# First feed-forward projection as seven block products, second projection in groups of 8, 7 and 7 tiles

## The chip, the cores and the metric

The kernel runs on one core of a Trainium2 chip. The metric is device time in microseconds, the median of several runs. TensorE is PE here (its weight loads PEld), VectorE is DVE, ScalarE is ACT, GpSimd is POOL, and SyncE is SP, which issues most loads.

## The reference, cut to what matters

One layer of a transformer trunk for 512 latent and 128 context tokens, 640 in all, with D_MODEL = 1024 and D_FF = 2816. The change concerns its last part, after attention and the output projection:

```python
h = modulate(x, norm2_w, shift2, scale2)          # (640, 1024)
a, up = jnp.split(h @ w_ffn_in, 2, axis=-1)       # 2 x (640, 2816)
a = dwconv3(a, ffn_conv_w, ffn_conv_b)            # three neighbouring tokens
x = x + gate2[:, None, :] * ((jax.nn.silu(a) * up) @ w_ffn_out)
```

gate2 is a sixth of `silu(c) @ w_ada + b_ada`; a last RMSNorm with final_norm_w follows.

## The kernel before, in words

Everything is float32. A product is made of three TensorE products: each operand is split into a high part (rounded to the type fp32r) and the low rest, and hi x hi, hi x lo and lo x hi are added up in PSUM (`mm3`, `proj`; all matmuls are issued in `mm`, line 142). A weight tile is loaded by SP into one of three buffers `raw` (128 x 1024 columns, 512 KB), cast on ACT into `whi` (line 125) and subtracted on DVE into `wlo` (line 126); there are four buffers of each. The function `wload` does this.

Channels lie on partitions, tokens on columns. The feed-forward part takes 22 tiles of 128 channels. For a tile `ffn_proj` makes two projections, a (`pfa`) and up (`pfu`): eight blocks of 128 rows of h, three hi/lo terms, two token halves of 320 columns, 48 matmuls each. Then `ffn_tile` copies a out of PSUM (line 1088), applies the convolution (one ACT pass, line 1089; four DVE steps, lines 1091 and 1093, for latent and context tokens apart), SiLU (1095), the product with up (1096), and splits the result into gh and gl (1097, 1098). After 11 tiles the second projection adds them up into five token tiles (`acc`), in two passes of 512 output columns, and DVE multiplies by the gate and adds to x (lines 1171, 1172). So there are two groups of 11 tiles. The last pass of the second group calls `finish`, which also makes the last norm and stores.

The gate for this (`gate2`, in the profile `acc_g`) is made beside the first group: 8 loads of 512 KB of w_ada through the same `raw` buffers, 32 DVE accumulations of 512 columns (line 221), two splits and eight matmuls; `ffn` calls one step of it after each tile.

Ahead of it stands the output projection (`out_steps`, `pso`), 48 matmuls of 512 columns for each of five token tiles. A token tile's rows are then gated, added, normalised (lines 1026 to 1031), transposed on PE and modulated (`modulate`: evictions on DVE and ACT at lines 1046 and 1044, cast and subtraction into `h2` at 1050 and 1051). PE's order there is written out by hand and kept (`pinned`): the last modulation, of tile 4, comes after the first two half projections of the feed-forward part, which need only the first 320 tokens. From then on (`pinned[0] = False`) the framework's scheduler orders PE too; the other engines' order it always chooses itself, at compile time, from its own estimates, and every engine runs its instructions in order.

Of the kernel before, what the change touches and what calls it, by code (L numbers as in the profile page):

```python
# [67 lines left out]
def trunk_kernel(ctx: ExitStack, tc: tile.TileContext, a: dict, o: list):  # L68
# [41 lines left out]
    def f(ap):  # L110
        return ap.bitcast(F32)
# [29 lines left out]
    def mm(out, s, m, start, stop):  # L141
        pin(nc.tensor.matmul(out, s, m, start=start, stop=stop))  # L142
# [65 lines left out]
    def ada_acc(pool, col, hf, name):  # L208
# [3 lines left out]
        acc = pool.tile([P, 2, 512], F32, tag="acc", name=f"acc_{name}{hf}", bufs=2)  # L212
# [26 lines left out]
    def rows_cols(pool, ps):  # L239

        rows = pool.tile([8, 512], F32, tag="n2rows", name="n2rows", bufs=1)
# [731 lines left out]
    h2 = mg  # L973
    tail = ctx.enter_context(tc.tile_pool(name="tail", bufs=1, reuse_waits="tile"))
    x2 = [tail.tile([P, D], F32, tag=f"x2_{t}", name=f"x2_{t}") for t in range(NT)]
    g2 = [tail.tile([P, D], F32, tag=f"g2_{c}", name=f"g2_{c}") for c in range(2)]

    def ffn_half(i, u):

        w = wcols(w_fi, u * FF + i * P, P, 0, KD, f"f{'au'[u]}{i}")  # L980
        ps = bank2(f"pf{'au'[u]}{i}")
        proj(ps, w, h2, KD, halves=(0,))
        return ps, w

    def ffn_proj(i, u):
        if (i, u) in early or i < 2:
            ps, w = early.get((i, u)) or ffn_half(i, u)
            proj(ps, w, h2, KD, halves=(1,))
            return ps
        w = wcols(w_fi, u * FF + i * P, P, 0, KD, f"f{'au'[u]}{i}")  # L990
        ps = bank2(f"pf{'au'[u]}{i}")
        proj(ps, w, h2, KD)
        return ps

    early = {}
    with tc.tile_pool(name="wo", bufs=1, reuse_waits="tile") as wo:
# [3 lines left out]
        woB = [wo.tile([P, 3, D], F32R, tag=f"woB{i}", name=f"woB{i}") for i in range(2)]  # L1000

        def wo_of(i, k):
            return woA[i][:, k, :] if k < 5 else woB[i][:, k - 5, :]

        for k in range(KD):
            raw = wpool.tile([P, 1024], F32, tag="raw", name=f"raw_wo{k}", bufs=3)
            nc.sync.dma_start(raw, w_out[k * P:(k + 1) * P, :])
            nc.scalar.copy(wo_of(0, k), raw)
            nc.vector.tensor_tensor(wo_of(1, k), raw, f(wo_of(0, k)), ALU.subtract)
# [22 lines left out]

        def modulate(t):
            c, ts, y = t // 4, slice(t * P, (t + 1) * P), Y2[t]
            h32 = wo.tile([P, KD, P], F32, tag="h32", name=f"h32_{t}", bufs=1)
# [11 lines left out]
            n = KD if t < NT - 1 else KD // 2  # L1047
            for k in range(0, KD, n):
                ks = slice(k, k + n)
                nc.scalar.copy(h2[0][:, ks, ts], h32[:, ks, :])  # L1050
                nc.vector.tensor_tensor(h2[1][:, ks, ts], h32[:, ks, :], f(h2[0][:, ks, ts]), ALU.subtract)
# [20 lines left out]
    fw = ffn.tile([P, D], F32, tag="fw", name="fw", bufs=1)  # L1072
    nc.gpsimd.dma_start(fw, a["final_norm_w"].unsqueeze(0).broadcast_to([P, D]))
    GRP = 11

    def gate2():
        for hf in range(2):
            for acc in ada_acc(ffn, 5 * D, hf, "g2"):
# [4 lines left out]
    def ffn_tile(i, gh, gl):  # L1083
        pa, pu = (ffn_proj(i, u) for u in range(2))
        av = ffn.tile([P, TOK], F32, tag="av", name=f"av{i}", bufs=1)
        cv = ffn.tile([P, TOK], F32, tag="cv", name=f"cv{i}")
        w = [vcol[:, V_CW + j * NF + i:V_CW + j * NF + i + 1] for j in range(3)]
        nc.scalar.copy(two(av), pa[:, :, :HALF])
        nc.scalar.activation(two(cv), pa[:, :, :HALF], AF.Identity, bias=vcol[:, V_CB + i:V_CB + i + 1], scale=w[1])
        for s0, s1 in ((0, LAT), (LAT, TOK)):  # L1090
# [111 lines left out]
```

## Time and profile before

| | |
|---|---|
| median of 3 runs | 1108.32 us (1105.19 to 1108.43) |
| the profiled execution | 1108.31 us, span 1106.5 us |
| granted PE clock, mean | 0.991 |
| output projection, with its modulations | 578 to 638 us |
| feed-forward part, to the last matmuls of the second projection | 638 to 1100 us |

The profile is of one execution. Busy times are of instructions of an engine; a matmul's end is modelled, and matmuls overlap, so the time of one is read from the distance of their starts. A stretch's table tells which engine is full there, the chain of waits which work ended last. DVE's and POOL's instructions that wait for each other inside show that as a longer duration, not as idle time.

### The profile page before, as it was taken

To read this page: it belongs to the slowest core of one execution; us is meant where nothing else is said; L and a number is where in the kernel's file an instruction comes from. 1 tells how busy PE (TensorE), PEld (TensorE's weight loads), DVE (VectorE), ACT (ScalarE), POOL (GpSimd) and SP (SyncE) were. 2 spreads that over 40 slices of the span, in tenths; PEclk is the share of its full clock that TensorE was granted. 3 is DMA by queue.
4 is the path that set the end of the run, shared out by engine and by line. 5 is a ranking of instruction groups with operands and counts; after the bars stand their busy time and mean duration, and the time that the engine had idled before them with its cause. 6 is when DMAs were issued, how large, how long until landed. Compare 5 with 4: busy or idle time off the path is not lost.

```text
span 1106.5 us, 16752 instructions
## 1 busy us (share of the span) xinstructions
PE 1071.1 (97%) x6811; PEld 1006.3 (91%) x6811; DVE 701.2 (63%) x1041; ACT 486.5 (44%) x783; POOL 163.0 (15%) x160
## 2 busy tenths in 40 slices
PE   6988999999999999999999999999999999999997
PEld 4787899999999999999998899999988999999886
DVE  5968988988877577787756567564414444444164
ACT  8636667667665552222334444333311233333133
POOL 4444324323222630000000000000000000000020
PEclk9898999999999999999999999999999999999999
DMA  9830212112111124555565024241222222222212
GB/s 311 228 97 27 84 32 65 48 37 66 41 42 58 55 81 152 171 156 150 153 220 161 1 80 141 86 133 58 86 76 76 87 77 76 77 77 68 67 39 95
DMA packets 128478, 106.10 MB, mean 96 GB/s; under 512 B 4173, under 2 KB 110205, under 8 KB 128402
## 3 DMA queue, kind: packets, MB, share of 16 engines
q1 hardware_dynamic: 126450, 101.93, 29.9%
q0 software_dynamic: 1232, 1.80, 0.8%
q8 instruction: 53, 0.87, 0.3%
q10 hardware_dynamic: 720, 1.31, 0.3%
q14 instruction: 23, 0.19, 0.1%
HBM read 101.36 MB, written 3.67 MB: 95 GB/s over the span
## 4 chain that ended last, share of the span: by engine, by line
PE 80%; DVE 11%; ACT 4%; issue 2%; SPq 1%; DMA 1%; ACTq 0%; DVEq 0%
PE pfa L142 14%; PE pfu L142 14%; PE acc L142 13%; PE ps_g L142 10%; PE psyb L142 5%; PE pso L142 5%; PE psk L142 3%; PE psu L142 3%; PE psya L142 3%; PE s L142 2%; PE po L142 2%; PE psq L142 2%; DVE nm L667 2%; PE psv L142 2%; PE pat L145 1%
## 5 line engine op out<-in xcount | busy, mean ns | idle before, releaser
L142 PE MATMUL pfu<-mg,whi_fu 128*128 128x320 f32 x704 | 134.1, 308 | 0.0
L142 PE MATMUL pfa<-mg,whi_fa 128*128 128x320 f32 x704 | 134.1, 308 | 0.0
L142 PEld LDWEIGHTS pfa<-mg,whi_fa 128*128 128x128 f32 x704 | 110.9, 188 | 0.4
L142 PEld LDWEIGHTS pfu<-mg,whi_fu 128*128 128x128 f32 x704 | 110.7, 188 | 0.0
L142 PE MATMUL acc<-whi_fo,gA 128*128 128x512 f32 (+1 forms) x336 | 100.9, 379 | 0.0
L142 PE MATMUL ps_g<-hT,whi_g 128*128 128x320 f32 x512 | 96.7, 311 | 0.0
L142 PE MATMUL pfu<-mg,wlo_fu 128*128 128x320 f32 x352 | 82.2, 307 | 0.0
L142 PE MATMUL pfa<-mg,wlo_fa 128*128 128x320 f32 x352 | 82.2, 307 | 0.0
L142 PEld LDWEIGHTS ps_g<-hT,whi_g 128*128 128x128 f32 x512 | 80.2, 188 | 2.0 <-issue 1.5
L126 DVE TENSOR_TENSOR wlo_fo<-raw_fo,whi_fo 128x1024 fp32r<-128x1024 f32 (+1 forms) x24 | 27.3, 1145 | 80.8 <-ACT whi_fo L125 80.8
L669 ACT ACTIVATE p<-s,nm 128x640 f32<-128x640 f32 (+1 forms) x80 | 56.6, 709 | 40.0 <-DVE nm L667 39.4
L142 PEld LDWEIGHTS acc<-whi_fo,gA 128*128 128x128 f32 x336 | 62.1, 188 | 12.1
L126 DVE TENSOR_TENSOR wlo_fa<-raw_fa,whi_fa 128x1024 fp32r<-128x1024 f32 x22 | 26.9, 1224 | 66.3 <-ACT whi_fa L125 66.3
L1176 POOL TENSOR_TENSOR x<-x,fw 128x512 f32<-128x512 f32 x5 | 6.9, 1372 | 419.0 <-ACT sq L1175 419.0
L142 PE MATMUL psv<-whi_v,hT 128*128 128x256 f32 x320 | 66.4, 288 | 0.0
L125 ACT CAST whi_fo<-raw_fo 128x1024 fp32r<-128x1024 f32 (+1 forms) x24 | 23.3, 978 | 96.3 <-PE acc L142 71.3
L667 DVE TENSOR_REDUCE nm<-s 128x1 f32<-128x640 f32 (+1 forms) x80 | 56.5, 709 | 12.4 <-PE s L142 11.0
L142 PE MATMUL acc<-wlo_fo,gA 128*128 128x512 f32 (+1 forms) x168 | 63.7, 379 | 0.0
L125 ACT CAST whi_fa<-raw_fa 128x1024 fp32r<-128x1024 f32 x22 | 23.1, 1050 | 84.8 <-PE pfa L142 61.7
L221 DVE SCALAR_TENSOR_TENSOR acc_g<-raw_g,silu,acc_g 128x512 f32<-128x512 f32 x64 | 44.5, 746 | 24.8 <-DMA raw_g<-in_w_ada_dram 24.7
L142 PEld LDWEIGHTS pfu<-mg,wlo_fu 128*128 128x128 f32 x352 | 59.4, 188 | 0.0
L142 PEld LDWEIGHTS pfa<-mg,wlo_fa 128*128 128x128 f32 x352 | 59.4, 188 | 0.0
(337 smaller groups left out, 2576.3 us busy)
## 6 DMA issues: line engine op xcount, KB each, us to landing
raw_fa<-in_w_ffn_in_dram SPq DMA_DIRECT2D x22, 512.0 KB
raw_fu<-in_w_ffn_in_dram SPq DMA_DIRECT2D x22, 512.0 KB
raw_fo<-in_w_ffn_out_dram SPq DMA_DIRECT2D x20, 512.0 KB
raw_g<-in_w_in_dram SPq DMA_DIRECT2D x16, 512.0 KB
raw_g<-in_w_ada_dram SPq DMA_DIRECT2D x16, 512.0 KB
araw_sh<-in_w_ada_dram SPq DMA_DIRECT2D x8, 512.0 KB
araw_sc<-in_w_ada_dram SPq DMA_DIRECT2D x8, 512.0 KB
raw_v<-in_w_in_dram SPq DMA_DIRECT2D x8, 512.0 KB
```

Source lines behind the costliest of these rows:

```text
L125: nc.scalar.copy(hi[:, :n], rv)
L126: eng.tensor_tensor(lo[:, :n], rv, f(hi[:, :n]), ALU.subtract)
L142: pin(nc.tensor.matmul(out, s, m, start=start, stop=stop))
L145: pin(nc.tensor.transpose(out, x, ident))
L221: nc.vector.scalar_tensor_tensor(acc[:, c, :], raw[:, ki, :], sc[:, c, 2 * u + ki:2 * u + ki + 1], acc[:, c, :], ALU.mult, ALU.add)
L667: nc.vector.tensor_reduce(nm[:, i:i + 1], s, AX.XY, ALU.max, negate=True)
L669: nc.scalar.activation(p.rearrange("p (b n) -> p b n", b=s.shape[1]), s, AF.Exp, bias=nm[:, i:i + 1], accum_out=z[:, i:i + 1])
L1176: nc.gpsimd.tensor_tensor(x2[t][:, hs], x2[t][:, hs], fw[:, hs], ALU.mult)
```

## The change

The matrix [a; up] x [two halves of h's 1024 rows] x [two token halves] is taken as a 2 x 2 block product by Strassen's method in Winograd's form: seven products of (128 channels) x (512 rows) x (320 tokens) for a tile of a and up together, in place of eight. The sums of token blocks (`e1` to `e4`) are made once, in `modulate`; `e1` and the plain blocks go to `h2`, the others to the new `hx`. The sums of weight blocks are made for every tile on POOL (`weights2`) and then split on ACT and DVE like plain weights: `sa` for products 5 and 6, `sb` for 3 and 7. Products 1, 6, 7 and 4 add into one PSUM bank of a tile, 5 and 3 into its other, and 2 has its own; between them parts are copied out. `raw` buffers of a and up are now held until the sums have read them. The split of a's own weights is on POOL for tiles 0 to 7 and on DVE after. PE's order stays written out by hand to the end: `pinned` is not reset. In a tile's turn the products are (i,1), (i,2), (i-1,7), (i,5), (i,6), (i-1,4), (i,3). The groups are 8, 7 and 7 tiles, so that a group's results fit into the eight slots of two buffers; the second projection makes six passes in place of four, with the same matmuls in all, and its first two blocks come ahead of the group's last two products. The gate's steps all fall into the first group. The last three rows of w_out (`woB`) now lie in three of the four weight buffers.

The core of the diff:

```diff
-        for n, (i, u) in enumerate(((0, 0), (0, 1), (1, 0))):
-            if n == 2:
-                modulate(NT - 1)
-            early[i, u] = ffn_half(i, u)
-        pinned[0] = False
+        def weights2(i, p):
+            if p == 1:
+                raw2[i] = raw_of(i, 0)
+                hl = split(raw2[i], *w_pair(f"a{i}"), nc.gpsimd if i < GROUPS[1][0] else nc.vector)
+                W2[i, 1], W2[i, 2] = [x[:, :4, :] for x in hl], [x[:, 4:, :] for x in hl]
+            elif p == 5:
+                ra, ru = (raw2.pop(i) if i != 2 else raw_of(i, 0)), raw_of(i, 1)
+                sa, sb = (pools["ffn"].tile([P, KD, P], F32, tag="s", name=f"s{j}_{i}") for j in range(2))
+                nc.gpsimd.tensor_tensor(sa[:, :4, :], ru[:, :4, :], ru[:, 4:, :], ALU.add)
+                nc.gpsimd.tensor_tensor(sa[:, 4:, :], sa[:, :4, :], ra[:, :4, :], ALU.subtract)
+                hl = split(sa, *w_pair(f"s{i}"), nc.vector)
+                W2[i, 5], W2[i, 6] = [x[:, :4, :] for x in hl], [x[:, 4:, :] for x in hl]
+                nc.gpsimd.tensor_tensor(sb[:, :4, :], ra[:, 4:, :], sa[:, 4:, :], ALU.subtract)
+                nc.gpsimd.tensor_tensor(sb[:, 4:, :], ra[:, :4, :], ru[:, :4, :], ALU.subtract)
+                raw2[i] = ru
+                hl = split(sb, *w_pair(f"t{i}"), nc.vector)
+                W2[i, 3], W2[i, 7] = [x[:, :4, :] for x in hl], [x[:, 4:, :] for x in hl]
+            elif p == 7:
+                hl = [pools["ffn"].tile([P, 4, P], F32R, tag=t, name=f"{t}_{i}", bufs=1) for t in ("uh", "ul")]
+                W2[i, 4] = split(raw2.pop(i)[:, 4:, :], *hl, nc.gpsimd)
+        def product(i, p):
+            weights2(i, p)
+            if p == 1:
+                PS[i] = bank2(f"pf{i}")
+            pa, pc = PS[i][:, 0, :HALF], PS[i][:, 1, :HALF]
+            pb = bank1(f"pb{i}")[:, :HALF] if p == 2 else None
+            out = {1: pa, 6: pa, 7: pa, 4: pa, 5: pc, 3: pc, 2: pb}[p]
+            (wh, wl), (ah, al) = W2.pop((i, p)), h_block(p)
+            for k in range(4):
+                for n, (w, x) in enumerate(((wh, ah), (wh, al), (wl, ah))):
+                    mm(out, w[:, k, :], x[:, k, :], p in (1, 2, 5) and k + n == 0, k == 3 and n == 2, p in (6, 7, 4, 3))
...
+        for i, p in ((0, 1), (0, 2), (1, 1)):
+            product(i, p)
+        modulate(NT - 1)
+        product(2, 1)
...
+            for i, p in ((1, 2), (0, 5), (0, 6), (1, 5), (0, 3), (1, 6), (0, 7), (1, 3), (0, 4), (2, 2), (1, 7), (2, 5),
+                         (2, 6), (1, 4), (2, 3)):
+                product(i, p)
+                if p == 3:
+                    next(later, None)
...
+        for i in range(start, first + size):
+            for j, p in ((i, 1), (i, 2), (i - 1, 7), (i, 5), (i, 6), (i - 1, 4), (i, 3)):
+                product(j, p)
+            if g == 0:
+                next(later, None)
+                next(later, None)
...
+        out2 = out2_steps(g, 0)
+        for p in (7, 4):
+            next(out2)
+            product(end, p)
```

And in `modulate`, for the columns past the first 320 (`h1` holds the first 320 in float32):

```diff
+            nc.vector.tensor_tensor(e1, b12, h1[:, :4, cs], ALU.subtract)
+            nc.gpsimd.tensor_tensor(e3, b22, b12, ALU.subtract)
+            split_to(h2[0][:, :4, c2], h2[1][:, :4, c2], e1)
+            nc.vector.tensor_tensor(e2, b22, e1, ALU.subtract)
+            nc.gpsimd.tensor_tensor(e4, h1[:, 4:, cs], e2, ALU.subtract)
+            split_to(h2[0][:, 4:, c2], h2[1][:, 4:, c2], b22)
+            split_to(hx[0][:, :, cs], hx[1][:, :, cs], e[:, 4:, :n])
```

`split` and `split_to` are a cast on ACT and a subtraction on the engine named (DVE for `split_to`). After product 2 the corner is copied on ACT and added to on DVE, after 5 and 6 a part is copied out on ACT, after 3 and 7 a part is added on DVE. The convolution follows product 3; the product with up and the split into gh and gl follow product 4.

## Rows read from the trace of the kernel before

**Rows 1.** The page: busy us, share of the span and instructions of each engine.

```profile
PE 1071.1 (97%) x6811; PEld 1006.3 (91%) x6811; DVE 701.2 (63%) x1041; ACT 486.5 (44%) x783; POOL 163.0 (15%) x160
```

**Rows 2.** Table by stretch: length, busy us of PE, PEld, DVE, ACT, POOL; clock.

```profile
578.00:638.00 60.00, 60.00 (x281) 49.44 (x280) 34.24 (x49) 26.44 (x42) 0.00 (x0) 1.00 0.29 94
652.00:795.00 143.00, 143.00 (x975) 142.63 (x974) 81.49 (x116) 56.23 (x70) 0.00 (x0) 1.00 0.34 104
795.00:870.50 75.50, 75.50 (x333) 62.00 (x332) 23.06 (x28) 13.11 (x15) 0.00 (x0) 1.00 0.24 77
```

**Rows 3.** Chain of waits from 638 us: start, length, engine, tile, line, matmuls.

```profile
795.00 75.50 PE acc L142 x330
870.50 6.99 PE pfa L142 x48
877.49 6.99 PE pfu L142 x48
```

**Rows 4.** Groups by line, 690 to 1107 us: count, busy us, mean ns, idle before.

```profile
L126 DVE TENSOR_TENSOR wlo_fa<-raw_fa,whi_fa 128x1024 fp32r<-128x1024 f32 x17 | 20.8, 1224 | 57.4 <-ACT whi_fa L125 57.4
L125 ACT CAST whi_fa<-raw_fa 128x1024 fp32r<-128x1024 f32 x17 | 17.9, 1051 | 72.6 <-PE pfa L142 53.9 <-PE acc L142 12.2 <-PE pfu L142 6.5
L1091 DVE SCALAR_TENSOR_TENSOR cv<-av,vcol,cv 128x511 f32<-128x511 f32 x19 | 14.3, 751 | 2.6 <-ACT cv L1089 2.3
L1088 ACT COPY av<-pfa 128x640 f32<-128x640 f32 x18 | 12.3, 686 | 0.0
L1098 DVE TENSOR_TENSOR gA<-cv,gA 128x640 fp32r<-128x640 f32 x13 | 10.6, 819 | 0.0
L1091 DVE SCALAR_TENSOR_TENSOR cv<-av,vcol,cv 128x127 f32<-128x127 f32 x19 | 6.6, 346 | 0.0
L125 ACT CAST whi_fo<-raw_fo 128x512 fp32r<-128x512 f32 x4 | 2.5, 624 | 22.7 <-PE acc L142 22.7
L1109 DVE TENSOR_TENSOR yr<-acc,g 128x512 f32<-128x512 f32 x4 | 2.8, 689 | 9.1 <-PE acc L142 9.0
```

**Rows 5.** Timeline of DVE and of POOL, 1063 to 1069 us: start, length.

```profile
1064.22 1.78 DVE L1172 TENSOR_TENSOR x<-x,yr 128x512 f32<-128x512 f32 x1
...
1066.92 1.81 DVE L1172 TENSOR_TENSOR x<-x,yr 128x512 f32<-128x512 f32 x1
...
1063.75 1.70 POOL L1176 TENSOR_TENSOR x<-x,fw 128x512 f32<-128x512 f32 x1 [413.19 <-ACT sq L1175]
1066.90 1.29 POOL L1176 TENSOR_TENSOR x<-x,fw 128x512 f32<-128x512 f32 x1 [1.44 <-ACT sq L1175]
```

**Rows 6.** Timeline of POOL and of DVE in the attention part, 167 to 172 us.

```profile
167.94 2.41 POOL L126 TENSOR_TENSOR wlo_k<-raw_k,whi_k 128x1024 fp32r<-128x1024 f32 x1 [13.40 <-ACT whi_k L125]
170.30 1.80 POOL L541 TENSOR_TENSOR ry_k<-ry_k,cos 128x512 f32<-128x512 f32 x1
...
169.56 0.80 DVE L697 TENSOR_TENSOR tl<-pat,th 128x640 fp32r<-128x640 f32 x1
...
171.07 1.05 DVE L675 TENSOR_TENSOR z<-z,neglam 128x1 f32<-128x1 f32 x1
```

**Rows 7.** Timeline of DVE after the output projection: token tile 4's last row step.

```profile
643.35 0.75 DVE L1031 TENSOR_SCALAR y<-x,rstd_n 128x1024 f32<-128x1024 f32 x1
```

**Rows 8.** Timeline of SP and of ACT: a load of 512 KB and its cast.

```profile
592.35 0.37 SPq L122 DMA_DIRECT2D raw_fu<-in_w_ffn_in_dram  x1
...
596.06 1.05 ACT L125 CAST whi_fu<-raw_fu 128x1024 fp32r<-128x1024 f32 x1 [2.85 <-DMA raw_fu<-in_w_ffn_in_dram]
```

**Rows 9.** Table by stretch, columns as in rows 2: a hole of PE.

```profile
80.00:82.00 2.00, 0.00 (x0) 0.00 (x0) 1.97 (x2) 0.65 (x1) 1.91 (x2) 1.00 0.01 3
...
84.00:86.00 2.00, 0.00 (x0) 0.00 (x0) 1.97 (x2) 1.23 (x2) 1.63 (x1) 0.50 0.00 0
...
88.00:90.00 2.00, 2.00 (x10) 2.00 (x9) 1.76 (x3) 1.06 (x3) 0.00 (x0) 0.50 0.00 0
...
92.00:94.00 2.00, 2.00 (x16) 2.00 (x15) 1.94 (x3) 0.90 (x2) 1.94 (x2) 1.00 0.04 12
```

More of the change, by code (lines that the diff above doesn't have):

```diff
@@ L139, in pin, with mm @@
             tc.keep_in_program_order(ins)
-    def mm(out, s, m, start, stop):
-        pin(nc.tensor.matmul(out, s, m, start=start, stop=stop))
+    def mm(out, s, m, start, stop, more=False):
+        pin(nc.tensor.matmul(out, s, m, start=start, stop=stop, skip_group_check=more))
     def tr(out, x):
@@ L239, in rows_cols @@
     def rows_cols(pool, ps):
-        rows = pool.tile([8, 512], F32, tag="n2rows", name="n2rows", bufs=1)
+        rows = wpool.tile([P, 1024], F32, tag="raw", name="raw_n2rows", bufs=3)[:8, :512]
         nc.vector.tensor_copy(rows, ps[:8, :])
@@ L970, in trunk_kernel, with h_block @@
                 more(2)
-    h2 = mg
     tail = ctx.enter_context(tc.tile_pool(name="tail", bufs=1, reuse_waits="tile"))
     x2 = [tail.tile([P, D], F32, tag=f"x2_{t}", name=f"x2_{t}") for t in range(NT)]
[L976 to L995, printed above, removed]
+    h2 = mg
+    hx = [tail.tile([P, 12, HALF], F32R, tag=f"hx{i}", name=f"hx{i}") for i in range(2)]
+    def h_block(p):
+        if p in (6, 7, 4):
+            k0 = {6: 0, 7: 4, 4: 8}[p]
+            return [x[:, k0:k0 + 4, :] for x in hx]
+        k0, c0 = {1: (0, 0), 2: (4, 0), 3: (4, HALF), 5: (0, HALF)}[p]
+        return [x[:, k0:k0 + 4, c0:c0 + HALF] for x in h2]
     with tc.tile_pool(name="wo", bufs=1, reuse_waits="tile") as wo:
@@ L1073, in trunk_kernel @@
-    nc.gpsimd.dma_start(fw, a["final_norm_w"].unsqueeze(0).broadcast_to([P, D]))
-    GRP = 11
+    pools["ffn"] = ffn
+    g2 = [ffn.tile([P, D], F32, tag=f"g2_{c}", name=f"g2_{c}", bufs=1) for c in range(2)]
     def gate2():
         for hf in range(2):
-            for acc in ada_acc(ffn, 5 * D, hf, "g2"):
+            for acc in ada_acc(ffn, 5 * D, hf, "g2", 1):
                 yield
@@ new lines, in trunk_kernel @@
+    later = gate2()
+    top_left(0)
+    for g, (first, size) in enumerate(GROUPS):
+        G2 = [res.tile([P, 8, TOK], F32R, tag=f"r{i}", name=f"g{g}{i}") for i in range(2)]
+        for j in range(size):
+            GT[first + j] = [x[:, j, :] for x in G2]
+        if g == 0:
[4 more added lines that the diff above has]
+                    next(later, None)
+            start = 3
+        else:
+            for p in (1, 2, 5, 6, 3):
+                product(first, p)
+            start = first + 1
+        for i in range(start, first + size):
+            for j, p in ((i, 1), (i, 2), (i - 1, 7), (i, 5), (i, 6), (i - 1, 4), (i, 3)):
+                product(j, p)
+            if g == 0:
+                next(later, None)
+                next(later, None)
+        if g == 0:
+            for _ in later:
+                pass
+            fw = ffn.tile([P, D], F32, tag="acc", name="fw", bufs=1)
+            nc.gpsimd.dma_start(fw, a["final_norm_w"].unsqueeze(0).broadcast_to([P, D]))
+        end = first + size - 1
+        out2 = out2_steps(g, 0)
+        for p in (7, 4):
+            next(out2)
+            product(end, p)
+        for hf in range(2):
+            for _ in out2 if hf == 0 else out2_steps(g, 1):
+                pass
```

195 lines of the change are left out of this document (122 added, 73 removed).

## The prediction

> **What bounds the kernel now.** I read the page first: PE is busy for 97% of the span, DVE for 63%, ACT for 44%, POOL for 15% [rows 1]. A share of the whole span can hide stages with other limits, so next comes the table by stretch [rows 2]: in the output projection, the feed-forward tiles and the second projection PE is busy without a hole at granted clock 1.00, while in the tiles DVE works 81 us of 143, ACT 56, and POOL nothing. The chain of waits says the same [rows 3]: 48 matmuls of 320 columns, one projection of one tile, take 6.99 us, and the next 48 start where they end. That is 145.6 ns a matmul. So a matmul less is 0.146 us less, as long as its weights come as fast as now. The sum is made against the profiled execution: 1108.3 us, of which 1106.5 are span; it stands at the median of the three runs (1108.32).
>
> **What the change removes.** A tile now needs 2 x 2 x 8 x 3 = 96 matmuls (a and u, two token halves, eight row blocks, three hi/lo terms); with seven block products it needs 7 x 4 x 3 = 84. Over 22 tiles that is 264 matmuls, 264 x 0.1456 = **38.4 us off the path**. A tile then lasts 84 x 0.1456 = 12.2 us on PE instead of 14.0.
>
> **What it adds, by engine, for one tile.** Durations from [rows 4]; for 320 columns I interpolate: DVE 0.49 us (0.69 at 512, 0.82 at 640), ACT 0.52 (0.62 and 0.69).
> - ACT: three casts of 1024 columns and one of 512 (3 x 1.05 + 0.62), three copies out of PSUM (1.6), then three passes over 640 columns (2.1): 7.5 us. It fits into 12.2.
> - DVE: two subtractions of 1024 (2.4), from tile 8 on three; the four convolution steps (2.2); one add of the corner and two into PSUM's pieces (1.5); two products of 320 (1.0); the subtraction for gl (0.8): 7.9 us, 9.1 from tile 8 on. In the first group the second gate adds 32 accumulations, 0.75 each like the step of 511 columns, and two subtractions of 1.22, 26 us over 8 tiles: 11.2 us a tile.
> - POOL, idle in these stretches now [rows 2]: four sums of 512 columns and one subtraction of 512, 5 x 1.29 = 6.45 us, and for tiles below 8 the subtraction of 1024 too, 2.41: 8.86 us (512 by [rows 5], 1024 by [rows 6]).
>
> Each engine alone fits. **Two of them together do not.** In [rows 5] POOL multiplies two SBUF operands for 1.29 us from 1066.90, to 1068.19; a DVE addition of two SBUF operands of 512 columns that starts at 1066.92 takes 1.81 us instead of 0.69 and ends 0.54 us after POOL. The one of 1064.22 ends 0.55 us after POOL's of 1063.75, which itself took 1.70. They take turns. In [rows 6] DVE takes one operand from PSUM beside a POOL subtraction and pays nothing (0.80 us for 640 columns), but a tiny addition of two SBUF operands waits 1.05 us for POOL. So I add POOL's time to that part of DVE's which has two SBUF operands, at about 1.04 us per 1000 columns: s and t splits, convolution, one product and gl are 4284 columns, 4.5 us; with the a split 5.5; the gate's 18432 columns are 19.2 us, 2.4 a tile. **First group: 8.9 + 4.5 + 2.4 = 15.7 us a tile; later groups: 6.45 + 5.5 = 12.0 us**, beside PE's 12.2.
>
> **The start.** PE's order is now fixed throughout, so it can fill a hole with nothing. Let E be the end of the output projection, 638.0.
> - The last token tile's rows are ready for transposing at E + 6.1 [rows 7]; the products placed ahead of it are (0,1), (0,2), (1,1), 36 x 0.146 = 5.2 us: 1 us of waiting, today hidden by 48 matmuls.
> - Product (0,5) needs the sum weights of tile 0. Three of four weight buffers hold the last rows of w_out until E; so a_1 and a_2 are split late, each with a cast of 1.05 and a POOL subtraction of 2.41, beside two POOL subtractions of the modulation: I put the end of a_2 at E + 6. Then its raw buffer takes u_0, which lands 3.7 us after its issue (592.35 to 596.06 [rows 8]): E + 9.7. Two POOL sums, a cast, a DVE subtraction, 4.9 us: E + 14.6. PE is there at E + 10.6 (5.2 + 1, an estimated 0.9 for eight transposes, and 3.5 for (2,1) and (1,2)): **4 us**.
> - Product (1,5) needs u_1, for which the buffer of a_0 must come free: after four POOL sums with some 2 us of turns, E + 17; lands E + 20.6; the sums, cast and subtraction again: E + 26.5. PE is there at E + 18.1: **8 us**.
> Together 13 us. Below: 4, if the buffers come free earlier. Above: 18, if the sum tiles also have to wait for memory of the modulation's last temporaries.
> Such holes cost twice. In [rows 9] PE stands still from 80 to 86 us; the granted clock falls to 0.50, the level of 1.2 GHz; it is still there from 88 to 90, with 10 matmuls in 2 us, and back at 92, with 16. That is some 5 us at half rate, 2.5 us lost; I take **2.5 us** (0 to 5). The Trainium skill, TensorE: Matmul & The Clock Gate, section Why this matters for your kernels, warns of just this, gaps between bursts of matmuls that put the clock back; by it both holes would pay, 5 us and a time of 1105, by the value taken 1102. The one hole of [rows 9] agrees with it.
>
> **The first group after its start.** Tiles 3 to 7 need 15.7 us of the shared path for 12.2 us of PE: 5 x 3.5 = 17 us if nothing helps. Two blocks of the second projection, 60 matmuls at 75.50 / 330 = 0.229 us [rows 3], 13.7 us, stand before the last two products and cover some of the tail. I take **10 us** (0 to 26; the upper end with POOL's and DVE's times added up whole, 11.2 + 8.9 less 1.6 of DVE's PSUM work less some overhead, 17 us a tile).
>
> **The later groups.** 12.0 of 12.2 us leaves no room for hand-overs or for a load of 3.7 us that waits for a raw buffer (three of them, each held until POOL has read it). I take 0.6 us for each of 12 tiles, the first of each group being prepared during the second projection: **7 us** (0 to 15).
>
> **At nothing.** Three modulations get up to 3.3 us more DVE work each and POOL subtractions, under out-projection matmuls, where DVE is busy 34 us of 60, ACT 26, POOL 0 [rows 2]; if that cover were gone it would be 8 us. The second projection keeps its matmul count and its loads; ten more evictions of two DVE steps (0.69 each) lie beside PE, DVE being busy 23 us of 75 there [rows 2]. fw's load moves from the start to the end of group 0, still long before its reader. The end of the kernel keeps its last block of six tiles.
>
> **Sum:** -38.4 + 13 + 2.5 + 10 + 7 = -5.9: **1102 us**.
>
> **Rivals.**
> - *Everything hides.* Preparations run a tile ahead, turns fall into idle time, the start costs 4 us. 1108.3 - 38.4 + 4 = **1074 us**. For it: each engine's own sum fits. Against: 15.7 against 12.2 in the first group is a sum of measured turns.
> - *The shared path decides: slower.* Place: POOL's queue between a raw load and the s weights, in group 0 and again in every tile. Price: start 18, clock 5, group 0 26, later groups 15, in all 64: 1108.3 - 38.4 + 64 = **1134 us**. It decides from the point where the four terms exceed 38.4. For it: the two rows of turns, three raw buffers, queues in fixed order, so that a late POOL sum delays DVE's subtraction and with it the evictions behind it. Against: PSUM work and POOL can overlap, and in the later groups the sum just fits.
> - *PE itself.* If 320-column matmuls of four row blocks came slower than of eight, the gain would shrink; the two halves already alternate between banks today, and nothing in [rows 3] speaks for it. I give it no chance of its own.
>
> **Chances.** Forecast 0.48 (its own range 1092 to 1112), all hidden 0.18 (1070 to 1086), shared path 0.34 (1108 to 1134). A measurement of this kernel tells a difference from none beyond about 0.3%, 3.3 us: faster is below 1105.0, slower above 1111.6. Faster: 0.18 and two thirds of the forecast's case, 0.32: 0.50. Same: the upper part of the forecast's case, 0.13, and a little of the third, 0.02: 0.15. Slower: 0.35. The range from 1074 to 1128 leaves out half of the first rival and the worst quarter of the second, about 0.18.
>
> **What would show it.** Right: 1848 matmuls of 320 columns instead of 2112; POOL busy some 160 us in the feed-forward part; DVE subtractions and accumulations of 1.2 and 0.75 us stretched to 2 us and more beside POOL; PE holes before (0,5) and (1,5) that end on a DVE subtraction of sum weights; few holes after tile 8. Wrong: PE without holes from 638 on (first rival); holes at every tile of all three groups with POOL near 90% (second rival); a granted clock below 0.95 for whole tiles; or waits that end on ACT or on PSUM evictions, which I cost at nothing.

## The result: 6.3% slower

The changed kernel takes 1176.63 us (median of 4 runs, 1173.12 to 1179.88) against 1106.84 beside it; the ratio is 1.063, 95% interval 1.059 to 1.067. I had forecast 1102 and given half the chance to faster. The profiled execution took 1179.9 us, span 1177.9, against a span of 1106.5 before: 71.4 us more. From the page of the changed kernel, the lines that answer to [rows 1], and the granted clock in 40 slices of 29.4 us:

```profile
PE 1066.8 (91%) x6535; PEld 987.1 (84%) x6535; DVE 821.7 (70%) x1175; ACT 539.3 (46%) x877; POOL 359.9 (31%) x285
...
PEclk9899999999999999999999787969999999999999
```

PE has 276 instructions fewer and is 9% idle instead of 3%. The table by stretch of the changed kernel (columns as in [rows 2]; the last two are the busy share of the DMA engines and the GB/s that they moved): output projection, start, the other tiles of group 0, then the tiles of groups 1 and 2.

```profile
584.30:643.00 58.70, 58.70 (x273) 48.24 (x272) 31.94 (x49) 22.34 (x41) 6.79 (x5) 1.00 0.18 63
643.00:680.00 37.00, 16.82 (x82) 15.08 (x80) 23.04 (x24) 12.38 (x21) 20.56 (x15) 0.74 0.15 43
680.00:813.50 133.50, 105.22 (x584) 99.24 (x585) 96.86 (x119) 55.92 (x79) 63.00 (x40) 0.84 0.31 95
871.70:965.00 93.30, 85.39 (x566) 82.26 (x565) 66.47 (x87) 47.16 (x66) 38.43 (x26) 1.00 0.24 71
1013.00:1111.00 98.00, 88.78 (x580) 85.08 (x579) 69.41 (x92) 48.02 (x67) 43.69 (x28) 1.00 0.23 68
```

The loss is mostly in group 0, and there no engine is full: in the third line DVE is busy for 73%, POOL for 47%, PE for 79% at clock 0.84. The pair of DVE and POOL has less room than these shares suggest: by the starts and ends of their instructions at least one of the two is busy for 119.4 of the 133.5 us, 89%. I use three marks for all that follows: **F**, the start of the first feed-forward matmul; **group 0**, from F to the first matmul of the second projection; **the rest**, from there to the last matmul of the second projection.

| | matmuls alone | changed kernel | lost |
|---|---|---|---|
| F | 638.0 (before) | 643.2 | 5.2 |
| group 0: 648 matmuls x 0.1456 + 0.9 for transposes | 95.2 | 170.3 | 75.1 |
| the rest: 151.3 of second projection + 171.2 (14 tiles x 84) + 3.5 (24 matmuls of tile 7) | 326.0 | 357.2 | 31.2 |

Together 111.5 lost, less the 38.4 gained, is 73.1; the spans differ by 71.4 (the kernel before takes 156.8 us for its first eleven tiles, some 2 us more than their matmuls alone). What PE waited for from 640 us to its last matmul: engine, tile and line, what ended the wait, us in total, times, longest.

```profile
PE pf L143 <- ACT whi_s L1088: 20.2, 5, 9.0
PE pf L143 <- ACT c L1141: 12.9, 21, 2.1
PE pf L143 <- ACT av L1143: 11.2, 11, 1.4
PE pt L146 <- DVE y L1029: 7.9, 1, 7.9
PE pf L143 <- DVE wlo_s L1089: 7.7, 6, 2.5
PE acc L143 <- DVE yr L1262: 5.7, 2, 3.6
```

`pf` is the PSUM tile of the products, `pt` that of the transposes, `acc` that of the second projection; `whi_s`, `wlo_s` are the sum weights of products 5 and 6, `c` the copy of product 5 out of PSUM, `av` that of product 6, `y` the last token tile's rows, `yr` evictions of the second projection. The second, third and last lines are waits that I had costed at nothing. In group 0 all waits of PE make up 48.5 us of the 75.1. The rest is slow matmuls: PE is busy for 16.8 + 105.2 us there, 26.8 more than the 95.2 counted at the upper clock.

**The start.** DVE's, then POOL's timeline of the changed kernel:

```profile
642.14 1.70 DVE L1063 TENSOR_TENSOR e<-h,h 128x512 f32<-128x512 f32 x1
643.77 1.27 DVE L1024 TENSOR_TENSOR y<-pso,acc_g 128x512 f32<-128x512 f32 x2
644.97 1.70 DVE L1066 TENSOR_TENSOR e<-h,e 128x512 f32<-128x512 f32 x1
646.59 1.79 DVE L1033 TENSOR_TENSOR mg<-e,mg 128x512 fp32r<-128x512 f32 x1
648.30 1.75 DVE L1033 TENSOR_TENSOR mg<-h,mg 128x512 fp32r<-128x512 f32 x1
649.97 1.21 DVE L1025 TENSOR_TENSOR x<-x,y 128x1024 f32<-128x1024 f32 x1
...
655.63 0.75 DVE L1029 TENSOR_SCALAR y<-x,rstd_n 128x1024 f32<-128x1024 f32 x1
```

```profile
640.89 5.23 POOL L1089 TENSOR_TENSOR wlo_a<-raw_fa,whi_a 128x1024 fp32r<-128x1024 f32 x2 [8.13 <-ACT whi_a L1088]
646.08 1.75 POOL L1064 TENSOR_TENSOR e<-h 128x512 f32<-128x512 f32 x1
...
666.06 1.26 POOL L1110 TENSOR_TENSOR s<-raw_fu 128x512 f32<-128x512 f32 x1
```

Between the gate product of token tile 4 (`y`, 643.77) and its addition to x (649.97), DVE's order holds three steps of tile 3's modulation, each stretched from 0.69 to 1.7 us beside POOL. The step that makes the rows starts 12.6 us after the output projection's last matmul (643.0), in [rows 7] it was 5.8 (after 637.6); POOL's first weight sum starts at 666.06, behind its block differences.

**Group 0 behind the start.** The chain of waits there, start, length, piece:

```profile
692.67 3.88 DMA raw_fu<-in_w_ffn_in_dram
696.71 1.30 POOL s L1110
698.07 1.40 issue
699.47 1.30 POOL s L1111
700.76 1.81 POOL ul L1089
702.58 2.24 POOL s L1114
704.84 4.55 DMA raw_fa<-in_w_ffn_in_dram
...
715.48 4.76 DMA raw_g<-in_w_ada_dram
720.30 1.02 issue
721.32 0.48 DVE av L1155
721.79 1.27 DVE acc_g L222
...
727.07 1.22 DVE wlo_s L1089
728.33 3.05 PE pf L143 x10
```

It passes through three loads one after the other (up weights, a weights, the gate's), through POOL and through DVE, where the split `wlo_s` stands behind the gate's accumulations, and only then reaches PE. The casts of the sum weights of tiles 2 to 7 start at 700.8, 724.2, 738.6, 764.9, 784.1 and 799.2 us: 19.7 us a tile on the mean. The groups by line of 643 to 813.5 us show turns in it (the mean in ns stands before the second bar; steps of these sizes took 751 and 1224 ns in [rows 4]):

```profile
L222 DVE SCALAR_TENSOR_TENSOR acc_g<-raw_g,silu,acc_g 128x512 f32<-128x512 f32 x32 | 29.5, 961 | 5.5 <-DMA raw_g<-in_w_ada_dram 5.5
...
L1089 DVE TENSOR_TENSOR wlo_s<-s,whi_s 128x1024 fp32r<-128x1024 f32 x8 | 11.8, 1473 | 3.8 <-ACT whi_s L1088 3.8
```

### The profile page after: what moved, and what is told of

The parts are those of the page before. It is cut to its first block, busy times and chain, and to the rows that moved or that the text cites. A ratio compares the mean times of both kernels' runs of the same rounds, so it can differ in the third digit from the quotient of the medians.

```text
span 1177.9 us, 16670 instructions
## 1 busy us (share of the span) xinstructions
PE 1066.8 (91%) x6535; PEld 987.1 (84%) x6535; DVE 821.7 (70%) x1175; ACT 539.3 (46%) x877; POOL 359.9 (31%) x285
## 3 DMA queue, kind: packets, MB, share of 16 engines
q1 hardware_dynamic: 127490, 102.45, 28.5%
## 4 chain that ended last, share of the span: by engine, by line
PE 60%; DVE 19%; ACT 6%; POOL 5%; issue 5%; DMA 4%; SPq 1%; ACTq 0%; POOLq 0%; DVEq 0%
PE acc L143 11%; PE pf L143 10%; PE ps_g L143 9%; PE psyb L143 5%; PE pso L143 4%; PE psk L143 3%; PE psu L143 2%; PE psya L143 2%; PE s L143 2%; DMA raw_fu<-in_w_ffn_in_dram 2%; PE po L143 2%; DVE nm L668 2%; PE psq L143 2%; PE psv L143 2%; DVE acc_g L222 1%
## 5 line engine op out<-in xcount | busy, mean ns | idle before, releaser
L143 PE MATMUL acc<-whi_fo,g 128*128 128x512 f32 (+1 forms) x454 | 140.0, 387 | 5.7 <-DVE yr L1262 5.7
L143 PEld LDWEIGHTS acc<-whi_fo,g 128*128 128x128 f32 x454 | 85.6, 191 | 23.2 <-DVE yr L1262 6.3
L143 PE MATMUL acc<-wlo_fo,g 128*128 128x512 f32 (+1 forms) x227 | 87.8, 387 | 0.0
L143 PE MATMUL pf<-mg,whi_s 128*128 128x320 f32 x176 | 43.5, 336 | 20.2 <-ACT whi_s L1088 20.2
L126 DVE TENSOR_TENSOR wlo_fo<-raw_fo,whi_fo 128x1024 fp32r<-128x1024 f32 (+1 forms) x24 | 28.3, 1180 | 47.8 <-ACT whi_fo L125 47.8
L143 PE MATMUL ps_g<-hT,wlo_g 128*128 128x320 f32 x256 | 59.0, 312 | 0.3 <-DVE wlo_g L126 0.3
L143 PE MATMUL pf<-hx,whi_s 128*128 128x320 f32 x176 | 46.1, 351 | 12.9 <-ACT c L1141 12.9
L143 PEld LDWEIGHTS psv<-whi_v,hT 128*128 128x128 f32 x320 | 53.4, 193 | 0.3 <-ACT whi_v L125 0.3
L1089 POOL TENSOR_TENSOR wlo_a<-raw_fa,whi_a 128x1024 fp32r<-128x1024 f32 x8 | 19.7, 2470 | 111.1 <-ACT whi_a L1088 111.1
L143 PE MATMUL s<-ks,qd 128*128 128x320 f32 x144 | 44.2, 318 | 10.4 <-DVE ks L579 7.1
L143 PE MATMUL pf<-mg,whi_t 128*128 128x320 f32 x176 | 40.1, 315 | 11.2 <-ACT av L1143 11.2
L143 PEld LDWEIGHTS acc<-wlo_fo,g 128*128 128x128 f32 x227 | 43.2, 191 | 8.2
```

Of the source, the lines that this page charges most:

```text
L126: eng.tensor_tensor(lo[:, :n], rv, f(hi[:, :n]), ALU.subtract)
L143: pin(nc.tensor.matmul(out, s, m, start=start, stop=stop, skip_group_check=more))
L1089: eng.tensor_tensor(lo, src, f(hi), ALU.subtract)
```

## The experiments

All runs stand in one table; each was timed beside the kernel before on its own chip. F, group 0 and the rest are from the profile. Since the framework's scheduler lays out the early part anew with every edit, F moves between 636 and 643 us, so the last two columns say more than the time.

| | us | before | ratio (95%) | F | group 0 | rest |
|---|---|---|---|---|---|---|
| changed kernel | 1176.6 | 1106.8 | 1.063 (1.059-1.067) | 643.2 | 170.3 | 357.2 |
| e1 groups only | 1107.5 | 1106.8 | 1.000 (0.998-1.003) | 637.8 | 114.8 (plain) | 346.9 |
| e2 no gate | 1147.3 | 1106.8 | 1.036 (1.030-1.042) | 639.5 | 147.2 | 354.3 |
| e3 no sums | 1134.6 | 1106.8 | 1.025 (1.021-1.028) | 639.6 | 138.1 | 349.1 |
| e4 own banks | 1159.5 | 1106.8 | 1.047 (1.042-1.052) | 641.1 | 165.8 | 345.2 |
| e5 plain blocks | 1161.9 | 1104.0 | 1.052 (1.042-1.062) | 643.3 | 156.7 | 357.1 |
| e6 e2+e3+e4 | 1103.8 | 1104.0 | 0.999 (0.997-1.000) | 641.2 | 120.2 | 333.5 |
| e7 e6+e5 | 1086.6 | 1104.0 | 0.984 (0.980-0.988) | 643.3 | 102.4 | 332.7 |
| e8 holes filled | 1175.3 | 1104.0 | 1.064 (1.059-1.069) | 643.3 | 167.2 | 357.0 |
| e9 sums on DVE | 1167.8 | 1106.8 | 1.056 (1.053-1.059) | 639.3 | 152.6 | 366.6 |
| e10 e5, rows own | 1155.3 | 1106.8 | 1.044 (1.041-1.048) | 636.2 | 155.2 | 356.2 |
| e11 e2, 4th raw | 1161.7 | 1106.8 | 1.050 (1.046-1.054) | 639.7 | 151.0 | 364.0 |
| e12 late gate | 1162.8 | 1106.8 | 1.051 (1.048-1.054) | 639.8 | 157.8 | 356.4 |
| e13 e2, early up | 1166.2 | 1106.6 | 1.054 (1.048-1.060) | 639.8 | 150.1 | 364.5 |
| e14 e13+e4 | 1129.0 | 1106.6 | 1.020 (1.017-1.023) | 639.6 | 138.6 | 342.5 |
| e15 combined | 1132.6 | 1106.6 | 1.023 (1.020-1.026) | 641.1 | 136.5 | 344.7 |
| e16 differences on DVE | 1169.7 | 1106.6 | 1.057 (1.054-1.060) | 638.4 | 166.2 | 356.8 |
| e17 e13, late Silu | 1165.6 | 1107.1 | 1.053 (1.050-1.056) | 639.8 | 149.8 | 366.6 |
| e18 combined further | 1126.9 | 1107.1 | 1.018 (1.015-1.021) | 639.4 | 133.1 | 344.9 |

**e1, the groups alone** (in the kernel before, `GRP = 11` becomes `GROUPS = ((0, 8), (8, 7), (15, 7))`, and the gate's steps are taken faster, so that they end with the first group).

> The kernel before with groups of 8, 7 and 7 tiles and nothing else changed. All theories: the second projection keeps its matmuls and loads, ten more evictions lie beside PE: within 3 us of 1106.8. If the grouping itself costs, through PSUM banks or the gate that now has to be ready after 8 tiles: 1112 or more.

The grouping costs nothing; its rest of 346.9 is just what its matmuls take, 326.0 + 14 x 12 x 0.1456 - 24 x 0.1456.

**e2, no gate**: `later = gate2()` becomes `later = iter(())`, g2 is set to ones.

> The changed kernel without the second gate: its 8 loads, 32 accumulations, splits and matmuls are left out, and the gate is set to ones. Theory of the turns (POOL's sums and DVE's steps with two SBUF operands share a path): the gate's 19 us of the shared path go, some 20 us off, 1156, and group 0 still lasts far over its 94 us of matmuls. Rival, the raw buffers (the gate's loads take the buffers that the weight sums need): 40 us or more off, 1136 or less, group 0 at some 115 us.

**e3, no sums**: `hl = split(sa, ...)` and `split(sb, ...)` take `ru` and `ra`.

> The changed kernel without the four weight sums of a tile: the raw a and up tiles are split in place of the sums; loads, casts, subtractions and matmuls stay. Theory of the turns: POOL keeps only the splits, most of the loss goes, 1100 or less. Rival, the raw buffers: they are still held till the split, loads still queue behind it, 30 us off at most, 1146. Rival, the PSUM banks (PE waits for copies out of its own tile's other bank): the waits of 24 us stay.

**e4, own banks**:

```diff
+            if p == 5:
+                PC[i] = bank1(f"pc{i}")
-            pa, pc = PS[i][:, 0, :HALF], PS[i][:, 1, :HALF]
+            pa, pc = PS[i][:, 0, :HALF], PC[i][:, :HALF] if i in PC else None
```

> The changed kernel with the bank of products 5 and 3 taken as a tile of its own, from the pool of single banks. In the trace PE waits 12.9 us in 21 places for the copy that follows product 5 and 11.2 us in 11 places for the copy that follows product 6, though the next product writes the other bank. Rival of the banks: these waits go, up to 24 us off, 1153. Theory of the turns: the time is set by the weights, the waits move elsewhere, 1170 to 1177.

Three real causes, none of which explains the loss alone; e2 and e3 both fall between their theories. Without sums it is still 2.5% slower, and of the 24 us of waits for the copies 15 stay; without the gate, group 0 is 23 us shorter and the later groups hardly change. The third is one that I had not thought of: PE, about to write one bank of a PSUM tile, waits for ACT to copy product 5 out of the *other* bank. In e4 the rest is 12 us shorter, and these are PE's longest waits from 640 us on (`pc` is the tile of its own):

```profile
PE pc L143 <- ACT whi_s L1088: 18.9, 4, 8.4
PE pc L143 <- DVE wlo_s L1089: 11.7, 6, 4.7
PE pf L143 <- DVE c L1150: 10.0, 8, 1.6
PE pt L146 <- DVE y L1029: 8.0, 1, 8.0
```

The waits for the ACT copies are gone. What is left, apart from weights, rows (`y`) and 5.3 us of evictions, is a wait for DVE's addition to `c`, which product 4 really needs. The Trainium skill, PSUM — Partial Sum Buffer, section PSUM bank collisions raise a hardware error, says that accesses must be kept apart by bank (and partition quadrant); e4 agrees that a wait between banks is not needed: it is the build's, made for the tile as a whole.

**e5, plain blocks**: `modulate` as before, and

```diff
-        if p in (6, 7, 4):
-            k0 = {6: 0, 7: 4, 4: 8}[p]
-            return [x[:, k0:k0 + 4, :] for x in hx]
+        k0, c0 = {..., 6: (0, HALF), 7: (4, 0), 4: (4, HALF)}[p]
```

> Left out: the differences of token blocks (three subtractions on DVE and POOL a tile and their splits) that the last three modulations now make; products 6, 7 and 4 take plain blocks instead, so the number and size of the matmuls is that of the changed kernel and the modulation is that of the kernel before. Theory A (the hole at the start comes from the modulation's extra work, its turns between DVE and POOL and its place in POOL's queue ahead of the first weight sums): the wait for the last token tile's rows falls from 8 us to under 3, product (0,5) starts 8 us or more earlier, the granted clock of 640 to 680 us rises, and the time falls by 15 to 25 us, to some 1152 to 1162. Theory B (the start waits for weights: the late splits of a_1 and a_2, the raw buffers): the wait for rows may shrink but (0,5) starts within 4 us of 674.7, and the time falls by less than 8 us.

**e6, e7**: e2, e3 and e4 together, then with e5.

> Left out: the second gate and the four weight sums (the raw a and up weights are split in their place); added: a PSUM tile of its own for products 5 and 3. One by one these took off 29, 42 and 17 us. Theory A (each is a cause of its own, and they add up): 1176.6 less 88, some 1085 to 1095. Theory B (they fill the same holes, behind a common start): little below the best single one, 1115 to 1130, with the start's hole and the low clock of 640 to 700 us unchanged.

> Left out: the second gate, the four weight sums and the differences of token blocks; added: the PSUM tile of its own for products 5 and 3. What is left of the change is its matmuls, the two grouped projections, the loads and splits. Theory A (with nothing beside them the matmuls give what was counted): 1106.8 less 38.4 and some 4 us of start, 1068 to 1076. Theory B (something else is in the way, the four weight buffers, the three raw buffers or the matmuls themselves): 1085 or more, with holes of PE that end on loads or splits in every tile.

e5: the wait for the last rows falls from 7.9 to 0.8 us, POOL's first sum starts at 652.8 instead of 666.1, and 14 us go, all in group 0. e6: 50 us less in group 0 and 24 in the rest, nearer to "they add up" (73 of the 88 us). e7 has the time of its theory B but not the holes in every tile. It shows that the matmuls give what I had counted: 17 of the 38.4 us are there, and 19 more are lost elsewhere, 5.3 by a later F, 7.2 in group 0 and 6.7 in the rest. The waits of PE over the whole feed-forward part are these:

```profile
PE acc L143 <- DVE yr L1239: 5.7, 2, 3.6
PE pt L146 <- ACT h L1043: 3.8, 1, 3.8
PE pt L146 <- DVE y L1026: 0.8, 1, 0.8
PE pc L143 <- DVE av L1132: 0.4, 1, 0.4
```

So the loss of group 0 divides, in this order of removal, into 50 for gate, sums and banks, 18 for the block differences, and 7 left; that of the rest into 24 for the same three and 7 left, of which 5.7 are evictions of the second projection.

**e8, the holes filled**: the 12 matmuls of product (1,1) are issued five times, those of (1,2) six times.

> Added: product (1,1) is multiplied five times and product (1,2) six times into the same bank, 48 matmuls in the hole before the last modulation's transposes (8 us) and 60 in the hole before (0,5) (9 us at the low clock). Nothing else is touched. Theory A (the holes cost a second time through the granted clock): the clock of 640 to 680 us goes from 0.6 to 0.7 up to 0.9 or more, the matmuls behind them run at full speed, and the time falls by 5 to 15 us. Theory B (the supply of weights sets the pace there, a faster TensorE only waits longer): the clock rises but the time stays within 4 us of 1176.6. If the holes were shorter than the filling, the time would rise by up to 8 us.

Table by stretch from 640 us in steps of 20, first e8, then the changed kernel:

```profile
640.00:660.00 20.00, 17.01 (x113) 16.02 (x112) 14.92 (x18) 8.27 (x15) 8.65 (x4) 1.00 0.10 27
660.00:680.00 20.00, 14.53 (x95) 13.48 (x94) 11.25 (x12) 7.32 (x11) 14.47 (x11) 1.00 0.18 53
```

```profile
640.00:660.00 20.00, 10.15 (x60) 9.01 (x59) 14.52 (x17) 8.09 (x14) 8.61 (x4) 0.85 0.09 27
660.00:680.00 20.00, 9.67 (x40) 8.61 (x38) 10.98 (x12) 7.18 (x11) 14.06 (x11) 0.67 0.18 53
```

The clock is at its upper level in these 40 us, 2.4 GHz, instead of falling toward 1.2; PE does 108 matmuls more; and the time is the same, as theory B has it. PE's speed there is worth nothing, since the weights come when they come.

**e9, sums on DVE**: `nc.gpsimd.tensor_tensor(sa/sb ...)` become `nc.vector`.

> The four weight sums go from POOL to DVE; nothing is left out. POOL keeps the a splits of group 0 and the subtraction of half of up. Theory A (turns between POOL and DVE are the price of the sums): a sum takes 0.69 us on DVE instead of 1.3 to 2.2 on POOL, DVE's other steps go back to their own length (the gate's accumulation from 0.85 to 0.75 us), and half or more of the 42 us that leaving the sums out gave come back: 1135 to 1155. Theory B (DVE's fixed order is what is full): 2.8 us more a tile stand in DVE's queue ahead of the splits, and the time stays above 1170.

Between the theories, and for a reason: group 0 gains 17.7 us, the rest loses 9.4, where DVE also has the a splits and the waits for the copy `c` rise from 12.9 to 28.5 us.

**e10, own rows**: e5, and `rows = pool.tile([8, 512], ..., tag="n2rows")` again as before.

> As in e5, the differences of token blocks are left out (products 6, 7 and 4 take plain blocks); and the transposed rows of the second norm's modulation lie in a tile of their own again, as in the kernel before, not in one of the three raw buffers. To be compared with e5 (1161.9 us; last output projection matmul at 643.1, in the kernel before at 637.6). Theory A (this part of the change holds a raw buffer back at 490 to 520 us: PE waits 3.2 us there for weights of the gate's projection, DMA moves 104 instead of 162 GB/s): that wait goes, the last output projection matmul starts at 638 to 639.5, and the time falls by 4 to 6 us, to 1156 to 1158. Theory B (the shift comes from the output projection's last rows of weights, which now share the weight buffers): no change, 1160 to 1164.

The same stretch in the changed kernel, then in e10:

```profile
480.00:520.00 40.00, 36.94 (x248) 35.53 (x246) 24.58 (x31) 9.12 (x12) 1.91 (x2) 1.00 0.35 104
```

```profile
480.00:520.00 40.00, 40.00 (x270) 38.95 (x269) 30.18 (x39) 9.18 (x10) 1.91 (x2) 1.00 0.53 159
```

Theory A: eight rows of 512 columns that borrow a raw buffer hold back the loads of another projection. The wait of 3.2 us there, for `whi_g`, is gone. F comes 7.1 us earlier than in e5, more than the theory said; how much of this is the buffer's isn't shown, since F lies anywhere from 638.4 to 643.3 in the runs that all borrow it.

**e11, a fourth raw buffer; e13, up split early** (both on e2).

```diff
+            if u and i >= 2 and i % 2 == 0:
+                raw = pools["ffn"].tile([P, KD, P], F32, tag="rawu", name=f"raw_fu{i}", bufs=1)
```

> As in e2 the second gate is left out (gate = ones); the room goes to a fourth raw buffer, for the up weights of every second tile from tile 2 on. To be compared with e2 (1147.3 us; 147.2 us from the first feed-forward matmul to the first of the second projection, 354.3 from there to the last). Theory A (from tile 3 on the pace is a loop of 13.8 to 14.6 us: POOL's four sums, the raw buffer that they free, the load of 4 to 5.5 us of the next up weights into it, the next sums): with one buffer more the load is a tile ahead, a tile takes 12.2 to 12.8 us, the rest falls from 354 to 335 to 340 and group 0 by 5 to 10 us; 1120 to 1132. Theory B (POOL's and DVE's time itself, turns included, or the waits for copies out of PSUM set the pace): less than 6 us, 1141 or more.

```diff
-            elif p == 7:
-                hl = [... for t in ("uh", "ul")]    # bufs=1
+                hl = [... for t in ("uh", "ul")]    # bufs=2, in the branch p == 5, ahead of sb's split
                 W2[i, 4] = split(ru[:, 4:, :], *hl, nc.gpsimd)
```

> As in e2 the second gate is left out (gate = ones); the room goes to a second pair of tiles for the split of the lower half of up, which is now made right after the sums of its own tile and not before product 7, inside the next tile. So the raw buffer of the up weights comes free earlier. To be compared with e2 (1147.3 us; 147.2 us in group 0, 354.3 from the first to the last matmul of the second projection). Theory A (the raw buffers set the pace of the later groups: load, four sums, late split, next load): the rest falls by 9 to 16 us, group 0 by up to 8; 1125 to 1138. Theory B (the sums' and splits' own time in the fixed queues of DVE, ACT and POOL, or the waits for copies out of PSUM, set the pace): the rest stays within 4 us of 354 and the time within 5 of 1147.

Both missed, and in the wrong direction: the rest became 10 us *longer*, and the waits for the copy `c` rose from 20.3 to 31.8 and 33.1 us. One tile of e13, ACT, then DVE and POOL of the same microseconds, and last the changed kernel's DVE group for comparison:

```profile
878.83 0.74 ACT L1167 ACTIVATE cv<-cv 128x640 f32<-128x640 f32 x1 [2.10 <-DVE cv L1165]
879.47 1.03 ACT L1088 CAST whi_s<-s 128x1024 fp32r<-128x1024 f32 x1
880.41 0.42 ACT L1139 COPY c<-pf 128x320 f32<-128x320 f32 x1
...
875.36 2.05 DVE L1163 SCALAR_TENSOR_TENSOR cv<-av,vcol,cv 128x511 f32<-128x511 f32 x2 [0.99 <-ACT cv L1161]
...
873.65 1.87 POOL L1114 TENSOR_TENSOR s<-raw_fa,s 128x512 f32<-128x512 f32 x1
875.49 1.78 POOL L1115 TENSOR_TENSOR s<-raw_fa,raw_fu 128x512 f32<-128x512 f32 x1
```

```profile
912.14 1.01 DVE L1165 SCALAR_TENSOR_TENSOR cv<-av,vcol,cv 128x511 f32<-128x511 f32 x2 [0.99 <-ACT cv L1163]
```

With the sums earlier, they meet the convolution: its first DVE group takes 2.05 us here, 1.01 in the changed kernel where POOL still waits for its load. ACT's Silu waits for it, the copy that PE needs stands behind the Silu and a cast in ACT's order, and a tile takes 14.8 us (PE restarts behind these copies at 880.88 and 895.66) against 14.0 in the changed kernel (903.39 and 917.35) and 13.8 in e2. By this reading, which is of one tile and which no run tests, a turn is paid by whatever stands behind the stretched step, and an earlier load only moves the turns.

**e12, late gate**: one step of the gate a tile in tiles 3 to 7, the rest after the blocks of the first second projection.

> Only the place of the second gate is changed: its first half is spread over tiles 3 to 7, its second half goes behind the blocks of the first second projection (DVE is busy there 4 to 10 us of 20). Theory A (the gate costs by standing in the feed-forward tiles: its accumulations wait in DVE's order for loads that share the three raw buffers, ahead of the weight splits): half or more of the 29 us come back, 1155 to 1165. Theory B (the 19 us of accumulations cost only by their sum with the other work of the group, or move the wait to the second projection, which waits for g2): less than 8 us, or a new hole before the first evictions.

Theory A in size: 13.8 of the 29 us come back, 12.5 of them in group 0, and nothing is lost behind it.

**e14**: e13 with e4.

> As e13 (second gate left out, early split of up), and products 5 and 3 in a PSUM tile of their own as in e4, where that alone took 12 us off the later groups. Theory A (raw buffers and PSUM copies are the two causes in the later groups): the rest comes to 331 to 336 us, 326 being its matmuls alone and 5.7 the waits for evictions; in all 1105 to 1120. Theory B (the sums' own time beside DVE sets the floor): the rest stays at 340 or more, as e4's 345.

Without the false waits for copies the rest is 342.5, 22 us below e13's, but above what the raw buffers should have left: theory A falls again and B holds. DVE stands without a gap for most of a tile, its convolution at twice its length beside POOL, and PE waits for its addition to `c`.

**e15, combined**: e4, e12, and e9's sums for tiles below 8 alone. **e16**: the two POOL differences in `modulate` on DVE. **e18**: e15 with e16 and the late Silu.

> Nothing is left out: products 5 and 3 in a PSUM tile of their own (e4), the second half of the gate behind the first second projection (e12), the weight sums of group 0 on DVE and of the later groups on POOL (e9's group 0 was 17.7 us shorter, its rest 9.4 longer). Theory A (separate causes): 1176.6 less 17, 14 and 18, about 1128. Theory B (they fill the same holes behind the common start): 1140 to 1152. By neither is it faster than the kernel before.

> The two differences of token blocks that POOL makes in each of the last three modulations go to DVE; nothing is left out. Theory A (the start suffers from POOL: turns that stretch DVE's steps there from 0.7 to 1.7 us, and POOL's queue, in which these differences stand ahead of the first weight sums): the wait for the last token tile's rows falls from 8 us to 4 or 5, POOL's first weight sum comes 3 us or more earlier than 666, and the time falls by 5 to 12 us. Theory B (the start suffers from the place of the work in DVE's order, ahead of the last tile's evictions): the wait stays at 7 us or more and the time within 4 us of 1176.6, or above.

> Nothing is left out: e15 (1132.6 us) with the token differences on DVE (e16, which took 7 us off by itself) and the late Silu (e17). Theory A (each of them takes off a wait of its own): 1120 to 1128. Theory B (group 0 is held by the weight sums and the gate whatever the start does, and in the later groups the own PSUM tile has already taken the copies out of the way): 1129 to 1136.

e15 and e18 come near the sum of their parts: 44 and 50 us of the 70 lost come back. Neither beats the kernel before. Of e16's 7 us some 4 are in group 0, the others an earlier F; the wait for the rows falls only to 6.3 us, POOL's first sum comes 12 us earlier, and PE meets the next hole instead.

**e17, late Silu**: `nc.scalar.activation(cv, cv, AF.Silu)` moves from `conv` to the head of `glu`.

> As e13 (second gate left out, early split of up), and the Silu of a tile is issued not at the end of its convolution but right before its product with up. So in ACT's order it stands behind the copies of the next tile's products 5 and 6, not ahead of them. To be compared with e13 (1166.2 us; group 0 150.1, rest 364.5; 33 us of waits for the copy of product 5, 1.6 to 2.4 each in the later groups). Theory A (turns stretch DVE's convolution beside POOL's sums from 1.0 to 2.05 us; ACT's Silu waits for it, and the copy that PE needs stands behind the Silu): these waits fall to some 0.5 to 1 us each, 15 us in all, and the rest to 345 to 354. Theory B (the pace is that of the sums and splits themselves): the waits only change their name, to the weights' casts, and the rest stays within 4 us of 364.

It told nothing: the scheduler put the Silu back to its old place, ahead of the cast and the copy, so ACT's order is e13's. Whether the copy's place in ACT's order can be mended is open.

## Why the prediction was wrong

- **The 264 matmuls: right.** 24 take 3.50 us, 145.8 ns each, and with the preparations gone (e7) the gain shows.
- **"The first group after its start", 10 us: the step that failed most.** With the start and the clock I had 25.5 us for group 0; it lost 75.1. Up to the first matmul of (1,5), at 684.57, PE took 41.4 us for 13.1 us of work: 28.3 lost, where I had 15.5 for start and clock. The 46.8 behind it stand against the 10. I added up DVE's and POOL's time to 15.7 us a tile, 17 at most, and took the sum for the pace; the measured pace is 19.7. DVE or POOL is busy for 89% of it, so the pair is not far from full, but its busy time holds the waits for each other, and 15.7 of 19.7 us is 80%. In the chain of waits the pace is the length of the way through load, sums, cast and split, in queues of fixed order, where each hand-over waits behind steps of other tiles. That reading is argued from the chain; no run separates it from a shared path that is nearly full. The turns are in it: the gate's accumulations have a mean of 0.96 us in group 0 instead of 0.75. But taking the sums' turns away (e9, which leaves the a splits on POOL) gave back 17.7, not the whole.
- **The start, 13 us.** Two holes were where I said, before the last transposes and before (0,5), but 7.9 and 9.0 us instead of 1 and 4; the third and largest, 8 us before (1,5), was 0.5, since PE came there 41 us after the output projection, where I had 18. The step that failed is "at nothing": tile 3's and 4's differences have no out-projection matmuls left to cover them, and they stand ahead of tile 4's own chain in DVE's and POOL's order. I had given 8 us "if that cover were gone"; e5 and e7 put it at 14 and 18. Two sums slipped as well: E + 20.6 and 4.9 us make E + 25.5, not 26.5, and five tiles of 17 us cost 24 us over PE's 12.2 each, not 26.
- **The clock, 2.5 us.** It fell further and for longer than I took: 0.74 until 680 us, 0.84 until 813. By the Trainium skill, TensorE: Matmul & The Clock Gate, section Why this matters for your kernels, both holes had to put the clock back. The rows agree: 0.85 and 0.67. Seen from PE, slow matmuls are 26.8 of the 75.1 us. Yet e8 shows that up to 680 us they cost nothing that can be measured: a slow PE that waits for weights loses no time. The stretch behind it, with some 20 of the 26.8, was not tested so.
- **The later groups, 7 us.** They lost 31.2. I had left out the copies out of PSUM, named only as what would make me wrong: 12 us for the banks alone (e4), 8 for the sums alone (e3), 24 together with the gate gone (e6), 5.7 for the second projection's evictions. The evictions wait in the changed kernel and in e7, not in e1, which has as many of them and leaves PE's order to the scheduler; why is open. With the 12.0 us of shared path that I found to "just fit", Strassen's tiles are no gain at all there: 357.2 against e1's 346.9 with 14 plain tiles.
- **Ahead of the start, nothing:** 5.2 us. One line of the diff that I never priced, the rows moved into a raw buffer, makes a wait of 3.2 us (e10); that the whole 5.2 is its work isn't shown.
- **The rivals.** The slower rival's place was right (POOL between a load and the sum weights), its price of 64 us was not: 111.5 were lost. It had every term from the same sum of engine time, so its upper ends were wrong together, and my range could not hold the result. The rival that all hides fell with the first hole.
- **The signs.** Two of those that I had named for being wrong came: a clock below 0.95 for whole tiles (0.84) and waits that end on copies out of PSUM.
- **Right:** the grouping costs nothing (e1).

Open: which single loop sets the 19.7 us of group 0 (raw buffers, scheduler's order, gate's loads), since gate, sums and banks overlap there; how much of its slow matmuls' 20 us is lost time; and whether another order on ACT and DVE would make the method pay.

## What to carry to other kernels

When a change trades matmuls for preparation, price the preparation as a chain, one tile from load to matmul through every queue with what stands ahead in each, and not as busy time per engine: DVE at 73% and POOL at 47%, one or the other at 89%, went with 19.7 us a tile instead of 12.2. Look for waits between an eviction and the next product in the same PSUM tile before tightening PE's order. And price every line of a diff that borrows a buffer from a ring, however small the data.

## What the runs showed of the hardware

A stretched step costs both engines: POOL's sums take up to 2.6 us instead of 1.29, and DVE's convolution 2.05 (e13) instead of 1.01 for the same pair of steps. The Trainium skill, SBUF — State Buffer, section SBUF: two separate sides, calls the pair of ports that DVE and GpSimd share an exclusive lock, which DVE's operations with two SBUF inputs take; these rows agree. And a granted clock of 0.67 over 20 us cost nothing that could be measured when the matmuls were waiting for weights anyway (e8).
